# Batch normalization of a product on one core: the order of the scale and shift broadcasts, the place of the affine terms, and the statistics of the last tile

## The chip, the cores and the metric

The kernel runs on 1 core of one Trainium2 chip. The metric is the device time of one execution in microseconds (us). A profiled execution also has a span, from its first to its last instruction; all times inside the program below are counted from the start of that span.

## The reference

```
x: (16, 512, 1024) f32   weight: (1024, 768) f32   gamma, beta: (768) f32   eps = 1e-5
y      = matmul(x, weight)                      # 8192 rows, 768 columns
mean   = mean(y over all rows);  var = var(y over all rows)      # per column
out    = gamma * (y - mean) / sqrt(var + eps) + beta             # f32
```

Nothing of the output can be written before all 8192 rows of a column have been multiplied, since mean and variance are taken over them. Written as `out = y * scale + shift`, each column needs two numbers: `scale = gamma / sqrt(var + eps)` and `shift = beta - mean * scale`.

## The kernel before, in words

**Tiling.** The 768 columns are six tiles of 128, numbered 0 to 5 (`nt`). The 8192 rows are sixteen chunks of 512 (`c`). Tiles 0 to 2 (`GA = 3`) are done together, in two layouts. In twelve chunks the rows stand on the partitions (`mm_rows`: 128 rows by 384 columns), and in the chunks `COLS = (0, 5, 10, 15)` the columns stand on the partitions (`mm`: 128 columns by 512 rows). Tiles 3 to 5 have columns on the partitions in all chunks; their first five chunks (`EARLY`) are multiplied while x is still being loaded, the other eleven after it.

**Stages.** Until about 127 us x is loaded, turned and multiplied for tiles 0 to 2. Then `affine_rows` works out scale and shift of tiles 0 to 2 on VectorE. For chunks in the row layout scale and shift have to lie along the free dimension, the same on all partitions: VectorE writes diagonal matrices (`affine_rows` those of scale, `shift_diag` those of shift), and `spread_rows(i)` multiplies a matrix of ones with them on TensorE. The result for `i = 0` stays in PSUM, that for `i = 1` is copied by ScalarE to `sum1`. Each pair of row blocks is then multiplied by scale on VectorE (`norm_rows`), shifted on GpSimd (`shift_rows`, which reads `sum1`) and stored (`store_rows`). Chunks with columns on the partitions are normalized in place in bf16 (`norm`, on VectorE or ScalarE), turned back by transposes on TensorE (`turn_y`, into `o_ps`), copied out by ScalarE (`out_copy`, into `ring` or, for tile 5, `o_sb`) and stored.

**Tiles 3 to 5.** While this goes on, TensorE multiplies the remaining eleven chunks of tile 3, then of tile 4, then of tile 5, in half units of four matmuls. Each unit of 512 rows is read twice from PSUM: `bn` takes its statistics on VectorE, `keep` copies it to SBUF in bf16 on ScalarE. After the last chunk of a tile `finish` makes scale and shift of it, and its sixteen chunks are normalized, turned and stored (`outputs`, `last_outputs`). A waiting list, `turns`, holds transposes: each matmul of `mm` is followed by one of them, and `out_copy` issues those still missing of its block.

**The last chunk of the last tile.** It is multiplied in two halves of 256 rows (`mm_half`), each with a PSUM bank, statistics (`bn_half`) and copy (`keep_half`) of its own. `sum_up` aggregates chunks 0 to 13 beforehand into the small tile `fin`, to which chunk 14 and the two halves add their records, so that `finish(5)` aggregates 21 numbers per partition.

**Order.** Every step is put down by `at(t, ...)` with a planned time t in us. The steps are then sorted by t, and `seq` ties each engine's instructions together in that order. So t is no time at which something runs: it sets only the order within each engine and within the queue of SP, which issues all stores. An instruction that waits holds everything behind it on its engine. `S` is the planned end of the first stage, `tr` the planned time of the next row pair, and `tk` that of the next chunk's transposes. The row pieces and output copies take their space one after another from `ring`, which has room for eight of 768 words.

Of the kernel before, what the change touches and what calls it, by code (L numbers as in the profile page):

```python
# [10 lines left out]
def kernel(  # L11
# [23 lines left out]
    nc = tc.nc  # L35
    f32 = mybir.dt.float32
    bf16 = mybir.dt.bfloat16
    AF = mybir.ActivationFunctionType
    ALU = mybir.AluOpType
# [5 lines left out]
    P = 128  # L45
    NT = N // P
    KQ = K // 4
    CH = 512
    RT = CH // P
    C = M // CH  # L50
    QR = 256
    QPC = CH // QR
    JW = KQ // 64
# [12 lines left out]
    singles = ctx.enter_context(tc.tile_pool(name="singles", bufs=1))  # L66
# [3 lines left out]
    psum = ctx.enter_context(tc.tile_pool(name="psum", bufs=8, space=bass.MemoryType.PSUM))  # L70
# [3 lines left out]
    def seq(bi):  # L74

        ins = bi.ins
        prev = last.get(ins.engine)
        if prev is not None:
            tc.add_manual_dep(
                ins, prev,  # L80
                mybir.DependencyInfo(mybir.DependencyClass.NoSync, mybir.DependencyReason.DATA),
                reason="order",
            )
        last[ins.engine] = ins.name
        return bi
# [4 lines left out]
    gamma_sb = singles.tile([P, NT], f32)  # L90
    beta_sb = singles.tile([P, NT], f32)
    scale = singles.tile([P, NT], f32)
    shift = singles.tile([P, NT], f32)
    ident = singles.tile([P, P], bf16)
    ring = singles.tile([P, RING], f32)
    w_sb = singles.tile([P, JW, 2, N], bf16)
    eps_sb = singles.tile([P, 1], f32)
# [10 lines left out]
    for acc in (sum1, sum2, sum3):  # L108
        seq(nc.vector.memset(acc, 0.0))
    stats = singles.tile([P, NT, C, 6], f32)  # L110
    fin = singles.tile([P, 21], f32)
    msq = singles.tile([P, GA], f32)
    mv = singles.tile([P, NT, 2], f32)
    std = singles.tile([P, NT], f32)
    tmp = singles.tile([P, NT], f32)
    rstd = singles.tile([P, 1], f32)
# [5 lines left out]
    xs, xT, py, ygrp, yrow, ops, ost, aff = {}, {}, {}, {}, {}, {}, {}, {}  # L122
# [168 lines left out]
    def y(nt, c):  # L291
        key, i = ((nt, c // GY), c % GY) if nt >= GA else ((0, c), nt)
        if key not in ygrp:
            y_sb = ypool.tile([P, GY, CH], bf16, tag="y")
            ygrp[key] = y_sb
        return ygrp[key][:, i]

    def bn(nt, c):
        if (nt, c) == (NT - 1, C - 2):
            seq(nc.vector.bn_stats(fin[:, 3:9], py[nt, c]))  # L300
            return
        i = c if nt >= GA else COLS.index(c)
        seq(nc.vector.bn_stats(stats[:, nt, i, :], py[nt, c]))  # L303

    def sum_up():

        seq(nc.vector.memset(fin[:, 0:1], float((C - 2) * CH)))
        seq(nc.vector.bn_aggr(fin[:, 1:3], stats[:, NT - 1, 0:C - 2, :]))
        seq(nc.vector.tensor_scalar(
            fin[:, 2:3], fin[:, 2:3], float((C - 2) * CH), None, op0=ALU.mult))  # L310

    def mm_half(q):
        y_ps = psum.tile([P, CH], f32, tag="b")
        py["half", q] = y_ps[:, 0:QR]
        for jw in range(JW):
            for e in range(2):
                seq(nc.tensor.matmul(  # L317
                    y_ps[:, 0:QR], w_sb[:, jw, e, (NT - 1) * P:NT * P],
                    xT[C - 1][:, jw, q * QR:(q + 1) * QR, e],
                    start=(jw == 0 and e == 0), stop=(jw == JW - 1 and e == 1),  # L320
                ))

    def bn_half(q):
        seq(nc.vector.bn_stats(fin[:, 9 + 6 * q:15 + 6 * q], py["half", q]))

    def keep_half(q):
        seq(nc.scalar.copy(y(NT - 1, C - 1)[:, q * QR:(q + 1) * QR], py.pop(("half", q))))

    def keep(nt, c):
        seq(nc.scalar.copy(y(nt, c), py.pop((nt, c))))  # L330

    def finish(nt):
        one = slice(nt, nt + 1)
        src = stats[:, nt, :, :] if nt < NT - 1 else fin
        seq(nc.vector.bn_aggr(mv[:, nt, :], src))
        seq(nc.scalar.activation(std[:, one], mv[:, nt, 1:2], AF.Sqrt, bias=eps_sb, scale=1.0))
        seq(nc.vector.scalar_tensor_tensor(
            tmp[:, one], mv[:, nt, 0:1], -1.0, gamma_sb[:, one], op0=ALU.mult, op1=ALU.mult,
        ))
        seq(nc.vector.reciprocal(rstd, std[:, one]))  # L340
        seq(nc.vector.tensor_mul(scale[:, one], rstd, gamma_sb[:, one]))
        seq(nc.vector.scalar_tensor_tensor(
            shift[:, one], tmp[:, one], rstd, beta_sb[:, one], op0=ALU.mult, op1=ALU.add,
        ))
# [51 lines left out]
    def at(t, fn, *args):  # L396
        events.append((t, len(events), fn, args))
# [31 lines left out]
    pe = 0.0  # L429
# [12 lines left out]
    def unit(nt, c, span, jws=range(JW)):  # L442
        nonlocal pe
        pe = max(pe, arrive[c * RT + RT - 1])
        at(pe, mm, nt, c, jws)
        pe += span
        if jws[-1] == JW - 1:
            at(pe + 0.2, bn, nt, c)
            at(pe + 1.0, keep, nt, c)
# [13 lines left out]
    pe = max(pe, arrive["w", 2])  # L463
# [15 lines left out]
            at(pe + 2.0, merge_rows)  # L479

    S = pe
    at(S + 0.9, affine_rows)
    at(S + 4.4, spread_rows, 0)
    for nt in range(GA):
        at(S + 2.4, norm, nt, 0, "dve")
    at(S + 2.5, shift_diag)
    at(S + 5.2, spread_rows, 1)
    ga = tuple(range(GA))
    tr, tk = S + 5.3, S + 3.9
    for c in range(C):  # L490
        if c in COLS:
            for nt in range(GA):
                if c:
                    at(tk - 3.4 + 0.8 * nt, norm, nt, c, "act")
            for s in range(0, RT, 2):
                at(tk + 0.7 * s, turn_y, ga, c * CH + s * P, 2)
                at(tk + 0.7 * s + 1.9, out_copy, ga, c * CH + s * P, "act")
                at(tk + 0.7 * s + 2.7, store, ga, c * CH + s * P, 2)
            tk += 9.6 if c else 8.6
        else:  # L500
            for s in range(0, RT, 2):
                at(tr, norm_rows, c, s)
                at(tr + 1.1, shift_rows, c, s)
                at(tr + 3.0, store_rows, c, s)
                tr += 1.85

    def outputs(nt, t0, step):
        for b in range(C // 2):
            tb = t0 + step * b
            for i in range(2):  # L510
                at(tb - 2.2 + 0.5 * i, norm, nt, 2 * b + i, "act" if tb < tr + 2.0 and i == 0 else "dve")
            at(tb, turn_y, (nt,), 2 * b * CH, 2 * RT)
            at(tb + 2.2, out_copy, (nt,), 2 * b * CH, "act")
            at(tb + 2.3, store, (nt,), 2 * b * CH, 2 * RT)

    def last_outputs(nt, t0):

        for c in range(C):
            tb = t0 + 0.6 * c
            at(tb - 1.2, norm, nt, c, "dve")  # L520
            at(tb, turn_y, (nt,), c * CH, RT)
            at(tb + 0.5, out_copy, (nt,), c * CH, "act", True)
            at(tb + 0.6, store, (nt,), c * CH, RT)

    halves = [range(JW // 2), range(JW // 2, JW)]
    for nt in range(GA, NT):
        for c in range(EARLY, C):
            if (nt, c) == (NT - 1, C - 1):
                for q in range(QPC):
                    at(pe, mm_half, q)  # L530
                    pe += 0.9
                    at(pe + 0.2, bn_half, q)
                    at(pe + (0.4 if q == 0 else 1.0), keep_half, q)
                at(pe - 2.4, sum_up)
                continue
            for jws in halves:
                unit(nt, c, MM_US / 2 + (0.12 if nt == GA else 0.17), jws)
        at(pe + 0.55, finish, nt)
        if nt == GA:
            outputs(nt, S + 41.0, 2.0)  # L540
        elif nt < NT - 1:
            outputs(nt, pe + 4.6, 1.85)
        else:
            last_outputs(nt, pe + 3.0)
# [39 lines left out]
```

## Time and profile before

| what | value |
|---|---|
| time, median of 3 runs (lowest to highest) | 223.25 us (222.83 to 223.74) |
| the profiled execution: its own time, and its span | 223.25 us, 221.5 us |
| TensorE matmul busy | 199.8 us (90%) |
| VectorE busy | 156.3 us (71%) |
| GpSimd busy | 134.4 us (61%) |
| ScalarE busy | 119.9 us (54%) |
| HBM read and written | 36.71 MB and 25.17 MB |

The profile is read so. PE is TensorE, DVE VectorE, ACT ScalarE, POOL GpSimd, SP the engine whose queue issues the stores. A line of a timeline gives the start and the duration in us, the engine, the line of the kernel, the operation, the tile written and the tiles read, and the count if alike instructions are merged (then the duration goes from the first start to the last end). In brackets stands the idle time of the engine before it and what ended it. A table of slices cuts the span into 40 equal parts of 5.5 us; each digit is a busy share in tenths. The busy share of an engine is an average over stages with different limits, so the stages are looked at one by one.

### The profile page before, as it was taken

To read this page: it belongs to the slowest core of one execution; us is meant where nothing else is said; L and a number is where in the kernel's file an instruction comes from. 1 tells how busy PE (TensorE), PEld (TensorE's weight loads), DVE (VectorE), ACT (ScalarE), POOL (GpSimd) and SP (SyncE) were. 2 spreads that over 40 slices of the span, in tenths; PEclk is the share of its full clock that TensorE was granted. 3 is DMA by queue.
4 is the path that set the end of the run, shared out by engine and by line. 5 is a ranking of instruction groups with operands and counts; after the bars stand their busy time and mean duration, and the time that the engine had idled before them with its cause. 6 is when DMAs were issued, how large, how long until landed. Compare 5 with 4: busy or idle time off the path is not lost.

```text
span 221.5 us, 3438 instructions
## 1 busy us (share of the span) xinstructions
PE 199.8 (90%) x1162; PEld 105.0 (47%) x1178; DVE 156.3 (71%) x268; ACT 119.9 (54%) x221; POOL 134.4 (61%) x153
## 2 busy tenths in 40 slices
PE   7997999999999999999999979999999988996600
PEld 2452455554544566646665534444444545654400
DVE  3221978886988789998554287889989999738500
ACT  2000463544543476646766225685766978986920
POOL 8787686878674799935569003999899951000000
PEclk9999999999999999999999999999999999999965
DMA  5999999999999999991000001886769899999996
GB/s 60 168 184 179 183 196 196 197 197 196 196 190 197 195 196 196 198 194 16 0 4 0 0 0 37 322 331 240 285 240 361 305 363 323 323 347 319 280 287 202
DMA packets 70161, 43.75 MB, mean 198 GB/s; under 512 B 4096, under 2 KB 69632, under 8 KB 70144
## 3 DMA queue, kind: packets, MB, share of 16 engines
q0 software_dynamic: 34624, 18.36, 60.7%
q1 hardware_dynamic: 35520, 25.18, 35.4%
q8 instruction: 9, 0.15, 0.3%
q14 instruction: 8, 0.07, 0.1%
HBM read 36.71 MB, written 25.17 MB: 279 GB/s over the span
## 4 chain that ended last, share of the span: by engine, by line
PE 63%; DVE 10%; POOL 8%; DMA 6%; issue 4%; ACT 3%; ACTq 0%; DVEq 0%; POOLq 0%
PE y_ps L191 30%; PE y_ps L181 28%; POOL ring L281 6%; PE o_ps L369 3%; ACT o_sb L382 3%; DMA w_sb<-in_weight_dram 3%; DVE stats L303 2%; DMA ring<-in_x_dram 2%; DVE ring L275 2%; DVE y_sb L353 2%; POOL w_sb L144 2%; DMA out_dram<-ring 1%; POOL ring L157 1%; PE y_ps L317 1%; PE a_ps L267 1%
## 5 line engine op out<-in xcount | busy, mean ns | idle before, releaser
L191 PE MATMUL y_ps<-xT_sb,w_sb 128*128 128x512 bf16 (+1 forms) x469 | 115.8, 382 | 2.6 <-DMA w_sb<-in_weight_dram 1.6
L191 PEld LDWEIGHTS <-w_sb 128*128 128x128 bf16 x484 | 46.2, 96 | 59.4 <-issue 2.6
L330 ACT CAST y_sb<-y_ps 128x512 bf16<-128x512 f32 x59 | 34.8, 590 | 54.2 <-DVE stats L303 52.3
L181 PE MATMUL y_ps<-w_sb,xT_sb 128*128 128x384 bf16 x384 | 63.4, 326 | 0.0
L281 POOL TENSOR_TENSOR ring<-ring,sum 128x768 f32<-128x768 f32 x24 | 43.6, 1844 | 17.9 <-ACT sum L269 14.0
L303 DVE BATCH_NORM_STATS2 stats<-y_ps 128x6 f32<-128x512 f32 x58 | 39.2, 684 | 19.9 <-PE y_ps L191 19.7
L157 POOL DMA_DIRECT2D ring<-in_x_dram x72 | 45.3, 635 | 12.5 <-DVE xT_sb L169 6.6
L181 PEld LDWEIGHTS <-xT_sb 128*128 128x128 bf16 x384 | 37.5, 98 | 25.6
L207 POOL TENSOR_TENSOR sum<-sum,sq_sb 128x384 f32<-128x384 f32 x38 | 38.3, 1007 | 18.0 <-ACT sq_sb L203 16.8
L169 DVE STREAM_TRANSPOSE xT_sb<-ring 128x1024 f32<-128x1024 f32 (+1 forms) x34 | 39.5, 1168 | 13.6 <-DMA ring<-in_x_dram 13.5
L369 PE MATMUL o_ps<-ident,y_sb 128*128 128x128 bf16 x240 | 37.2, 219 | 4.8 <-DVE y_sb L353 4.6
L210 DVE TENSOR_TENSOR sum<-y_ps,sum 128x384 f32<-128x384 f32 x48 | 26.1, 544 | 14.2 <-ACT sq_sb L203 13.4
L203 ACT ACTIVATE sq_sb<-y_ps 128x384 f32<-128x384 f32 x48 | 23.4, 492 | 15.0 <-PE y_ps L181 11.8
L216 ACT CAST y_sb<-y_ps 128x384 bf16<-128x384 f32 x48 | 22.8, 476 | 7.8 <-DVE sum L210 7.4
L382 ACT CAST ring<-o_ps 128x1024 f32<-128x1024 bf16 (+1 forms) x24 | 22.4, 952 | 4.9 <-PE o_ps L369 3.2
L369 PEld LDWEIGHTS <-y_sb 128*128 128x128 bf16 x240 | 19.1, 97 | 9.7 <-DVE y_sb L353 6.5
L275 DVE TENSOR_TENSOR ring<-y_sb,a_ps 128x768 f32<-128x768 bf16 x24 | 22.4, 939 | 0.2 <-PE a_ps L267 0.2
L353 DVE TENSOR_SCALAR y_sb<-y_sb,scale,shift 128x512 bf16<-128x512 bf16 x43 | 17.3, 460 | 0.0
L348 ACT ACTIVATE y_sb<-y_sb,shift,scale 128x512 bf16<-128x512 bf16 x17 | 13.3, 813 | 0.1
L150 PE MATMUL idle_ps<-idle_sb 128*128 128x512 bf16 x37 | 11.2, 473 | 1.2 <-DVE idle_sb L100 1.2
L382 ACT CAST o_sb<-o_ps 128x512 f32<-128x512 bf16 x16 | 7.9, 673 | 1.2 <-PE o_ps L369 1.2
L150 PEld LDWEIGHTS <-idle_sb 128*128 128x128 bf16 x38 | 4.3, 117 | 7.5 <-issue 3.8
(54 smaller groups left out, 42.3 us busy)
## 6 DMA issues: line engine op xcount, KB each, us to landing
ring<-in_x_dram POOLq DMA_DIRECT2D x56, 256.0 KB, 8.6
out_dram<-ring SPq DMA_DIRECT2D x32, 384.0 KB, 2.9
out_dram<-ring SPq DMA_DIRECT2D x16, 512.0 KB, 5.9
out_dram<-o_sb SPq DMA_DIRECT2D x16, 256.0 KB, 3.6
ring<-in_x_dram POOLq DMA_DIRECT2D x16, 128.0 KB, 5.4
w_sb<-in_weight_dram POOLq DMA_DIRECT2D x8, 96.0 KB, 4.7
w_sb<-in_weight_dram POOLq DMA_DIRECT2D x4, 192.0 KB, 5.9
gamma_sb<-in_gamma_dram SPq DMA_DIRECT2D x6, 0.5 KB, 4.7
```

Source lines behind the costliest of these rows:

```text
L157: seq(nc.gpsimd.dma_start(x_bf[32 * i:32 * i + 32], src[:, :, KQ * i:KQ * (i + 1)]))
L169: seq(nc.vector.transpose(dst[:, half, :, jw0:jw1], src[:, :, jw0:jw1]))
L181: seq(nc.tensor.matmul(y_ps, xT[c][:, jw, s * P:(s + 1) * P, e], w_sb[:, jw, e, 0:NA], start=(jw == 0 and e == 0), stop=(jw == JW - 1 and ...
L191: seq(nc.tensor.matmul(y_ps, w_sb[:, jw, e, nt * P:(nt + 1) * P], xT[c][:, jw, q0 * QR:q1 * QR, e], start=(jw == 0 and e == 0 and q0 == 0) ...
L207: seq(eng.tensor_add(acc, acc, py.pop(("sq", c, s))))
L210: seq(nc.vector.tensor_add(sum1, py["row", c, s][:, 0:NA], sum1))
L275: seq(nc.vector.tensor_mul(o_sb, yrow[c][:, s:s + 2], aff[0][:, None, :].to_broadcast([P, 2, NA]),))
L281: seq(nc.gpsimd.tensor_add(o_sb, o_sb, sum1[:, None, :].to_broadcast([P, 2, NA])))
L303: seq(nc.vector.bn_stats(stats[:, nt, i, :], py[nt, c]))
L330: seq(nc.scalar.copy(y(nt, c), py.pop((nt, c))))
L369: seq(nc.tensor.transpose(dst, src, ident))
L382: seq(nc.scalar.copy(o_sb, src))
```

## The change

Three things are changed. First, around `S`: `shift_diag` comes before the normalization of chunk 0 in VectorE's order, the two broadcasts `spread_rows` have only one half unit of products between them, the transposes of chunk 0 come after both, row products and shifts are planned 0.6 us earlier, and the transposes of the other chunks in `COLS` 1.0 us later. Second, `finish` of tiles 3 and 4 (the fourth and fifth) is split: `finish_var` does the aggregate, the square root and the reciprocal, and `finish_affine` works out scale and shift in three operations on ScalarE, planned 1.05 us behind it. They use the negated gamma, made once beforehand by `negate_gamma`. Third, the last chunk of the last tile is multiplied, read and kept as one unit like the others, and `finish(5)` aggregates sixteen records; `fin`, `sum_up` and the three functions for halves are gone. One consequence is not seen in the diff: `outputs` gives a normalization to ScalarE only while its planned time is under `tr + 2.0`, and with the smaller `tr` chunk 2 of tile 4 goes to VectorE.

```diff
--- before.py
+++ after.py
@@ -108,7 +108,8 @@
     for acc in (sum1, sum2, sum3):
         seq(nc.vector.memset(acc, 0.0))
     stats = singles.tile([P, NT, C, 6], f32)
-    fin = singles.tile([P, 21], f32)
+    ngamma = singles.tile([P, NT], f32)
+    nscale = singles.tile([P, 1], f32)
     msq = singles.tile([P, GA], f32)
     mv = singles.tile([P, NT, 2], f32)
     std = singles.tile([P, NT], f32)
@@ -296,43 +297,31 @@
         return ygrp[key][:, i]
 
     def bn(nt, c):
-        if (nt, c) == (NT - 1, C - 2):
-            seq(nc.vector.bn_stats(fin[:, 3:9], py[nt, c]))
-            return
         i = c if nt >= GA else COLS.index(c)
         seq(nc.vector.bn_stats(stats[:, nt, i, :], py[nt, c]))
 
-    def sum_up():
-
-        seq(nc.vector.memset(fin[:, 0:1], float((C - 2) * CH)))
-        seq(nc.vector.bn_aggr(fin[:, 1:3], stats[:, NT - 1, 0:C - 2, :]))
-        seq(nc.vector.tensor_scalar(
-            fin[:, 2:3], fin[:, 2:3], float((C - 2) * CH), None, op0=ALU.mult))
-
-    def mm_half(q):
-        y_ps = psum.tile([P, CH], f32, tag="b")
-        py["half", q] = y_ps[:, 0:QR]
-        for jw in range(JW):
-            for e in range(2):
-                seq(nc.tensor.matmul(
-                    y_ps[:, 0:QR], w_sb[:, jw, e, (NT - 1) * P:NT * P],
-                    xT[C - 1][:, jw, q * QR:(q + 1) * QR, e],
-                    start=(jw == 0 and e == 0), stop=(jw == JW - 1 and e == 1),
-                ))
-
-    def bn_half(q):
-        seq(nc.vector.bn_stats(fin[:, 9 + 6 * q:15 + 6 * q], py["half", q]))
-
-    def keep_half(q):
-        seq(nc.scalar.copy(y(NT - 1, C - 1)[:, q * QR:(q + 1) * QR], py.pop(("half", q))))
-
     def keep(nt, c):
         seq(nc.scalar.copy(y(nt, c), py.pop((nt, c))))
 
+    def negate_gamma():
+        seq(nc.vector.tensor_scalar(ngamma, gamma_sb, -1.0, None, op0=ALU.mult))
+
+    def finish_var(nt):
+        one = slice(nt, nt + 1)
+        seq(nc.vector.bn_aggr(mv[:, nt, :], stats[:, nt, :, :]))
+        seq(nc.scalar.activation(std[:, one], mv[:, nt, 1:2], AF.Sqrt, bias=eps_sb, scale=1.0))
+        seq(nc.vector.reciprocal(rstd, std[:, one]))
+
+    def finish_affine(nt):
+        one = slice(nt, nt + 1)
+        seq(nc.scalar.activation(nscale, rstd, AF.Identity, scale=ngamma[:, one]))
+        seq(nc.scalar.activation(scale[:, one], rstd, AF.Identity, scale=gamma_sb[:, one]))
+        seq(nc.scalar.activation(
+            shift[:, one], mv[:, nt, 0:1], AF.Identity, bias=beta_sb[:, one], scale=nscale))
+
     def finish(nt):
         one = slice(nt, nt + 1)
-        src = stats[:, nt, :, :] if nt < NT - 1 else fin
-        seq(nc.vector.bn_aggr(mv[:, nt, :], src))
+        seq(nc.vector.bn_aggr(mv[:, nt, :], stats[:, nt, :, :]))
         seq(nc.scalar.activation(std[:, one], mv[:, nt, 1:2], AF.Sqrt, bias=eps_sb, scale=1.0))
         seq(nc.vector.scalar_tensor_tensor(
             tmp[:, one], mv[:, nt, 0:1], -1.0, gamma_sb[:, one], op0=ALU.mult, op1=ALU.mult,
@@ -479,14 +468,15 @@
             at(pe + 2.0, merge_rows)
 
     S = pe
+    at(S - 30.0, negate_gamma)
     at(S + 0.9, affine_rows)
+    at(S + 2.4, shift_diag)
     at(S + 4.4, spread_rows, 0)
+    at(S + 5.6, spread_rows, 1)
     for nt in range(GA):
-        at(S + 2.4, norm, nt, 0, "dve")
-    at(S + 2.5, shift_diag)
-    at(S + 5.2, spread_rows, 1)
+        at(S + 5.0, norm, nt, 0, "dve")
     ga = tuple(range(GA))
-    tr, tk = S + 5.3, S + 3.9
+    tr, tk = S + 4.7, S + 6.3
     for c in range(C):
         if c in COLS:
             for nt in range(GA):
@@ -496,7 +486,7 @@
                 at(tk + 0.7 * s, turn_y, ga, c * CH + s * P, 2)
                 at(tk + 0.7 * s + 1.9, out_copy, ga, c * CH + s * P, "act")
                 at(tk + 0.7 * s + 2.7, store, ga, c * CH + s * P, 2)
-            tk += 9.6 if c else 8.6
+            tk += 9.6 if c else 7.2
         else:
             for s in range(0, RT, 2):
                 at(tr, norm_rows, c, s)
@@ -525,17 +515,13 @@
     halves = [range(JW // 2), range(JW // 2, JW)]
     for nt in range(GA, NT):
         for c in range(EARLY, C):
-            if (nt, c) == (NT - 1, C - 1):
-                for q in range(QPC):
-                    at(pe, mm_half, q)
-                    pe += 0.9
-                    at(pe + 0.2, bn_half, q)
-                    at(pe + (0.4 if q == 0 else 1.0), keep_half, q)
-                at(pe - 2.4, sum_up)
-                continue
             for jws in halves:
                 unit(nt, c, MM_US / 2 + (0.12 if nt == GA else 0.17), jws)
-        at(pe + 0.55, finish, nt)
+        if nt < NT - 1:
+            at(pe + 0.55, finish_var, nt)
+            at(pe + 1.6, finish_affine, nt)
+        else:
+            at(pe + 0.55, finish, nt)
         if nt == GA:
             outputs(nt, S + 41.0, 2.0)
         elif nt < NT - 1:
```

## The prediction

> **What bounds the kernel now.** I read the page first, then the busy time by stage, the timelines of TensorE, VectorE, GpSimd and ScalarE from 125 us on, and the stores at the end. The page, rows of slices:
>
> ```profile
> PE   7997999999999999999999979999999988996600
> DVE  3221978886988789998554287889989999738500
> ACT  2000463544543476646766225685766978986920
> POOL 8787686878674799935569003999899951000000
> PEclk9999999999999999999999999999999999999965
> DMA  5999999999999999991000001886769899999996
> ```
>
> Each digit is 5.5 us. TensorE is full from slice 1 to slice 35 with dips, at a full clock, so until the last products (201.1 us) the kernel runs at TensorE's pace; after that only stores are left. The change touches nothing of weight before 127 us. So the question is where TensorE stands still after 127 us, and what follows its last product. TensorE's timeline (start, us, operation, in brackets the idle time before it and its releaser):
>
> ```profile
> 130.53 0.39 PE L191 MATMUL y_ps<-xT_sb,w_sb 128*128 128x512 bf16 x1
> 132.10 0.23 PE L369 MATMUL o_ps<-ident,y_sb 128*128 128x128 bf16 x1 [1.19 <-DVE y_sb L353]
> ...
> 180.78 0.23 PE L369 MATMUL o_ps<-ident,y_sb 128*128 128x128 bf16 x1 [0.68 <-DVE y_sb L353]
> ...
> 184.02 0.68 PE L369 MATMUL o_ps<-ident,y_sb 128*128 128x128 bf16 x5 [0.60 <-DVE y_sb L353]
> ```
>
> All three waits are a transpose standing in TensorE's order before VectorE has normalized its tile: 1.19 + 0.68 + 0.60 = 2.47 us. Matmul ends are modelled; by the pitch of matmuls (0.23 us from start to start) the losses are 1.34, 0.85 and 0.76, together 2.95. I take the recorded 2.47 and keep 2.95 as the other end. VectorE's timeline at the ends of tiles 3 and 4 shows why it is late at the second and third:
>
> ```profile
> 152.13 0.59 DVE L335 BATCH_NORM_AGGREGATE mv<-stats 128x2 f32<-128x96 f32 x1
> 152.76 0.16 DVE L337 SCALAR_TENSOR_TENSOR tmp<-mv,gamma_sb 128x1 f32<-128x1 f32 x1
> 153.08 0.16 DVE L340 RECIPROCAL rstd<-std 128x1 f32<-128x1 f32 x1 [0.17 <-ACT std L336]
> 153.28 1.42 DVE L341 TENSOR_TENSOR scale<-rstd,gamma_sb 128x1 f32<-128x1 f32 x1
> ...
> 174.64 1.18 DVE L337 SCALAR_TENSOR_TENSOR tmp<-mv,gamma_sb 128x1 f32<-128x1 f32 x1
> 175.75 0.15 DVE L340 RECIPROCAL rstd<-std 128x1 f32<-128x1 f32 x1
> 175.93 1.69 DVE L341 TENSOR_TENSOR scale<-rstd,gamma_sb 128x1 f32<-128x1 f32 x1
> 177.54 0.21 DVE L342 SCALAR_TENSOR_TENSOR shift<-tmp,rstd,beta_sb 128x1 f32<-128x1 f32 x1
> ...
> 179.15 1.90 DVE L353 TENSOR_SCALAR y_sb<-y_sb,scale,shift 128x512 bf16<-128x512 bf16 x2
> ```
>
> Operations on one element per partition take 0.16 us, or 1.2 to 1.7. GpSimd's own timeline:
>
> ```profile
> 155.78 21.83 POOL L281 TENSOR_TENSOR ring<-ring,sum 128x768 f32<-128x768 f32 x12 [1.09 <-DVE ring L275]
> 178.75 1.82 POOL L281 TENSOR_TENSOR ring<-ring,sum 128x768 f32<-128x768 f32 x1 [1.14 <-ACT y_sb L348]
> ```
>
> Its adds end every 1.82 us: 155.78 + 11 x 1.82 = 175.80, where the stalled `tmp` ends (175.82); 177.61, where the stalled `scale` ends (177.62). The two normalizations at 179.15 take 1.90 us for a usual 0.72, and finish just after the add that ends at 180.57. So some VectorE operations stand until GpSimd's add is through. The reciprocal does not: 0.16 us at 153.08, inside an add. From 166 to 190 us VectorE has no idle time, so these stalls reach the transposes.
>
> The end, in steps of 0.55 us from 200 us, and the first store of the last tile on SP's queue:
>
> ```profile
> GB/s 362 326 334 344 350 345 346 342 55 202 296 290 293 299 279 308 290 286 292 276 302 285 286 294 267 303 284 283 292 269 301 283 287 288 288 271 33 0 0 0
> ...
> 204.23 13.31 SPq L387 DMA_DIRECT2D out_dram<-o_sb  x16
> ```
>
> Tile 4's stores drain at 204.4; 0.6 us is nearly empty; then 16 stores run at some 288 GB/s to 219.8, and the span ends at 221.5. What sets the end is thus the first store of the last tile, as long as tile 4's drain stays ahead of it.
>
> **The change part by part.** The sum is made against the profiled execution: 223.25 us, span 221.5, 1.75 around it. It equals the median of the runs shown (223.25), so it needs no correction.
>
> *Head, 127 to 137 us.* Chunk 0's transposes go behind both broadcasts; TensorE instead does three more products of its half unit (to 131.44) and the first broadcast, whose diagonal is ready at 130.85. The 1.19 wait is gone if nothing else is late. VectorE, by present pitches: statistics to 131.65, shift diagonals (0.59) to 132.24, statistics (0.61) to 132.85, the first row product (0.86) to 133.71, three normalizations (0.32 each) starting at 133.71, 134.02 and 134.34. TensorE: broadcast 131.44 to 132.08 (0.64, as from 134.91 to 135.55), a half unit to 132.99, the second broadcast to 133.63, a half unit without transposes to 134.54; the first transpose is at 134.77, after its input (134.05). **Minus 1.19.**
>
> What is near: GpSimd's first add starts 1.40 us after the second broadcast now (134.91, 136.31), so at 134.39, against 134.34 for the third normalization. If the add comes first, that normalization waits. From the pair at 179.15 (the next instruction starts at 180.96, less 2 x 0.33 gives 180.30, 0.27 before the add's recorded end) it gets through at about 135.9 and ends at 136.2, with the third transpose due at 135.3: 0.9 us. I take 0, since VectorE is ahead by the rows, and keep 0.9.
> The Trainium skill, "SBUF — State Buffer", section "Who interferes with whom", says that a VectorE `tensor_scalar` in its two-port mode and a GpSimd instruction exclude each other, and that whoever issues first blocks the other for its whole instruction. The trace agrees on the block but shows it ending some 0.3 us before the recorded end. By the rule the wait would be to 136.2 and cost 1.2 instead of 0.9; this speaks against putting the normalizations next to the first add.
>
> *GpSimd.* Its first add moves from 136.31 to about 134.4, 1.9 us earlier. Its idle 1.09 at 155 us waits for a row product behind the stalled `scale`. With 24 adds at 1.82 from 134.4 it ends near 178.1 instead of 183.8, if rows come in time; the row stores follow. That frees DMA time before tile 4's stores.
>
> *Tiles 3 and 4.* On VectorE, aggregate to the next row product is now 152.13 to 154.76 = 2.63 us and 174.03 to 177.67 = 3.64. What remains is aggregate, the square root's wait and the reciprocal: 152.13 to 153.28 = 1.15 us each. It saves 1.48 and 2.49. VectorE also takes one normalization over from ScalarE (tile 4, chunk 2; it falls below the changed limit on `tr`): plus 0.33. Net 2.2 us at tile 4, and fewer stalls after GpSimd's earlier end. TensorE's 0.68 and 0.60 are both smaller than that. **Minus 1.28**; bounds 0 and minus 1.61 by pitch. ScalarE takes three one-element operations per tile: the square root (0.30, next start after 0.19) is the nearest row, so 0.6 to 0.9 per tile. At tile 4 the normalization given away (0.81) pays for it; at tile 3 ScalarE idled 1.50 before the square root. Nothing. If that cover is gone, 0.9 falls on the output copies.
> Behind the square root on ScalarE are a copy to SBUF, the affine terms, a normalization and an output copy; behind the reciprocal on VectorE the next row product.
>
> *Last tile.* TensorE's time for the last unit does not change (eight of 0.23 against sixteen of 0.11). Statistics of 512 columns are 0.69 instead of 0.43, the aggregate of 16 records 0.58 instead of 0.25. Both lie on the path to the first store. **Plus 0.59.** `sum_up` was hidden: nothing. Transposes, copies and stores are as before.
>
> *Small edits.* `negate_gamma` (0.15) at about 97 us lies in a stage that TensorE sets: nothing, at most 0.15. Chunks 5, 10 and 15 are turned one half unit later in the order, which TensorE's earlier arrival offsets; SP's queue then sees row stores earlier relative to theirs. DMA is at 53% to 87% in most slices there, so nothing, bounds minus 0.3 and plus 0.3.
>
> *Drain.* The first late store moves 1.88 earlier, data from 205.0 to 203.1. Tile 4's drain, 204.4, must come 1.3 earlier. The head alone moves everything by 1.19, and 3 to 4 row stores of 384 KB (about 1.1 us each at 345 GB/s) leave the time after 177 us. I take it as met.
>
> Sum: -1.19 - 1.28 + 0.59 = **-1.88**, 223.25 to **221.4 us**. By pitch -1.34 - 1.61 + 0.59 = -2.36, 220.9.
>
> **The rivals.** *Race at the head lost:* the add takes the port first, 0.9 of the gain goes: -1.0, 222.3. For it: 0.05 us of lead. Against: both sides share most of their history.
> *Second half does not pay:* TensorE meets the waits again, or the drain stays at 204.4 (then only the empty 0.6 is won): -1.19 + 0.59 = -0.60, or -0.6: 222.65. For it: ScalarE and DMA are both full from 186 to 196 us. Against: ScalarE's idle 0.66, 0.39 and 0.93 between 179 and 186 wait for VectorE's statistics and go with it.
> *Slower: the square root holds ScalarE's queue at tile 4.* Ahead of the aggregate VectorE now has a normalization, which an add can hold by 1.5, and a row product (0.86, formerly behind). Then the aggregate ends near 175.8 and ScalarE, ready at 174.0, stands 1.8 us; after square root, reciprocal, copy, affine terms, normalization and output copy, tile 4's first normalization ends at 179.7 instead of 178.6. TensorE then is 1.1 later than before, plus 0.59: +1.7, 224.9. It decides once that normalization ends later than 178.6. Against: the present stalls of the normalizations from 168 to 174 are under 0.1.
>
> **How the numbers follow.** A measurement here can tell about 0.5% (1.1 us) from no change. Forecast 0.58, with its own range 220.8 to 222.2; race lost 0.16; second half 0.13; slower 0.13. Faster takes nearly all of the forecast and the better end of the first rival: 0.62. Same: 0.25. Slower: 0.13. The range 220.7 to 223.3 takes in the forecast and the two middle rivals.
>
> **What would show it.** Right: no idle over 0.3 us before L369 near 132 to 136 and 178 to 184; GpSimd's first add near 134.4 and its last ending before 180; reciprocal at tile 4 within 1.3 us of the aggregate's start; last product near 198.6; 2.2 us from there to the first normalization (1.6 now). Wrong: a normalization of 1.5 us near 134; idle before the square root with output copies behind it; a drain that ends after 203.2.

## The result, and the profile after

The changed kernel takes 225.91 us (median of 6 runs, 225.01 to 226.85) against 223.15 us before: a ratio of 1.012, 95% interval 1.0091 to 1.0149. It is slower, by more than the 0.5% that can be told from no change. The profiled execution took 225.01 us with a span of 223.2 us, the lowest of the six; it is compared with the profiled 221.5 us of before, so it explains 1.7 us of the 2.8.

TensorE's timeline of after, only the instructions that waited:

```profile
175.04 0.23 PE L358 MATMUL o_ps<-ident,y_sb 128*128 128x128 bf16 x1 [0.50 <-DVE y_sb L342]
...
177.96 0.23 PE L358 MATMUL o_ps<-ident,y_sb 128*128 128x128 bf16 x1 [0.50 <-DVE y_sb L342]
...
181.48 0.23 PE L358 MATMUL o_ps<-ident,y_sb 128*128 128x128 bf16 x1 [2.23 <-ACT y_sb L337]
```

The wait of 1.19 us at the head is gone, as forecast. The two waits at tile 4 (0.68 and 0.60) have become three, of 0.50, 0.50 and 2.23. VectorE's timeline of after shows where they come from:

```profile
166.31 2.83 DVE L342 TENSOR_SCALAR y_sb<-y_sb,scale,shift 128x512 bf16<-128x512 bf16 x1
169.07 0.94 DVE L276 TENSOR_TENSOR ring<-y_sb,a_ps 128x768 f32<-128x768 bf16 x1
169.93 0.68 DVE L301 BATCH_NORM_STATS2 stats<-y_ps 128x6 f32<-128x512 f32 x1
170.54 1.53 DVE L342 TENSOR_SCALAR y_sb<-y_sb,scale,shift 128x512 bf16<-128x512 bf16 x1
171.99 0.94 DVE L276 TENSOR_TENSOR ring<-y_sb,a_ps 128x768 f32<-128x768 bf16 x1
...
173.46 1.52 DVE L342 TENSOR_SCALAR y_sb<-y_sb,scale,shift 128x512 bf16<-128x512 bf16 x1
...
176.38 1.53 DVE L342 TENSOR_SCALAR y_sb<-y_sb,scale,shift 128x512 bf16<-128x512 bf16 x1
...
178.69 0.58 DVE L311 BATCH_NORM_AGGREGATE mv<-stats 128x2 f32<-128x96 f32 x1
```

Before, these four normalizations of tile 3 took 0.40, 0.45, 0.45 and 0.40 us. The first two of them in VectorE's timeline of before:

```profile
168.18 0.40 DVE L353 TENSOR_SCALAR y_sb<-y_sb,scale,shift 128x512 bf16<-128x512 bf16 x1
...
169.97 0.45 DVE L353 TENSOR_SCALAR y_sb<-y_sb,scale,shift 128x512 bf16<-128x512 bf16 x1
```

GpSimd's timeline of after, beside VectorE's:

```profile
134.65 34.34 POOL L282 TENSOR_TENSOR ring<-ring,sum 128x768 f32<-128x768 f32 x19 [12.06 <-ACT sum L270]
170.09 1.83 POOL L282 TENSOR_TENSOR ring<-ring,sum 128x768 f32<-128x768 f32 x1 [1.09 <-DVE ring L276]
173.01 1.83 POOL L282 TENSOR_TENSOR ring<-ring,sum 128x768 f32<-128x768 f32 x1 [1.09 <-DVE ring L276]
```

Nineteen adds run without a pause. The normalization issued at 166.31 waits for the running one and lets one more pass. It ends at 169.14, when GpSimd has nothing left. From then on the engines take turns: row product (0.86), add, and a normalization that stands until the add is nearly through. A round takes 2.92 us (from 170.09 to 173.01) where TensorE needs 2.25. The aggregate of tile 4 comes at 178.69, formerly at 174.03, and on ScalarE:

```profile
179.30 0.29 ACT L312 ACTIVATE std<-mv,eps_sb 128x1 f32<-128x1 f32 x1 [3.53 <-DVE mv L311]
...
180.62 0.80 ACT L337 ACTIVATE y_sb<-y_sb,shift,scale 128x512 bf16<-128x512 bf16 x1
```

ScalarE stands 3.53 us before the square root; behind it in ScalarE's order is the normalization of 180.62, for which TensorE waits 2.23 us. By the planned times that is chunk 8 of tile 3: it needs nothing of tile 4, and stands behind the square root only by the order.

The sum of the profiled executions: the stage begins 0.27 later (the last statistics of the load stage start at 127.37, formerly 127.10), head -1.19, tile 4 +3.23 - 1.28 = +1.95, together +1.03; the last product ends 1.14 later (202.21 and 201.07). From there to the first normalization it is 2.24 instead of 1.64: +0.60. That makes 1.74, against 1.7 of span.

### The profile page after: what moved, and what is told of

Its sections match the earlier page's. It is cut to its first block, busy times and chain, and to the rows that moved or that the text cites. A ratio compares the mean times of both kernels' runs of the same rounds, so it can differ in the third digit from the quotient of the medians.

```text
span 223.2 us, 3421 instructions
## 1 busy us (share of the span) xinstructions
PE 199.1 (89%) x1154; PEld 103.9 (47%) x1170; DVE 156.2 (70%) x260; ACT 119.0 (53%) x225; POOL 134.2 (60%) x153
## 4 chain that ended last, share of the span: by engine, by line
PE 73%; DVE 8%; DMA 5%; ACT 4%; issue 3%; POOL 3%; DVEq 0%; ACTq 0%; POOLq 0%
PE y_ps L192 40%; PE y_ps L182 28%; DVE y_sb L342 3%; PE o_ps L358 3%; ACT o_sb L371 3%; DMA w_sb<-in_weight_dram 3%; DMA ring<-in_x_dram 2%; DVE ring L276 2%; DVE stats L301 2%; POOL w_sb L145 2%; POOL ring L158 1%; PE a_ps L268 1%; PE tot_ps L228 1%; ACT y_sb L337 0%; ACT y_sb L304 0%
## 5 line engine op out<-in xcount | busy, mean ns | idle before, releaser
L192 PE MATMUL y_ps<-xT_sb,w_sb 128*128 128x512 bf16 (+1 forms) x477 | 117.8, 382 | 3.5 <-DMA w_sb<-in_weight_dram 2.4
L192 PEld LDWEIGHTS <-w_sb 128*128 128x128 bf16 x492 | 46.9, 96 | 61.6 <-issue 4.3
L304 ACT CAST y_sb<-y_ps 128x512 bf16<-128x512 f32 x60 | 35.3, 588 | 54.0 <-DVE stats L301 52.1
L301 DVE BATCH_NORM_STATS2 stats<-y_ps 128x6 f32<-128x512 f32 x60 | 40.5, 685 | 21.3 <-PE y_ps L192 20.7
L358 PE MATMUL o_ps<-ident,y_sb 128*128 128x128 bf16 x240 | 36.7, 219 | 6.3 <-DVE y_sb L342 3.7
L342 DVE TENSOR_SCALAR y_sb<-y_sb,scale,shift 128x512 bf16<-128x512 bf16 x44 | 22.5, 569 | 0.0
L337 ACT ACTIVATE y_sb<-y_sb,shift,scale 128x512 bf16<-128x512 bf16 x16 | 12.6, 813 | 0.0
L151 PE MATMUL idle_ps<-idle_sb 128*128 128x512 bf16 x37 | 10.4, 445 | 1.2 <-DVE idle_sb L100 1.2
```

The costliest lines, as they stand in the source:

```text
L192: seq(nc.tensor.matmul(y_ps, w_sb[:, jw, e, nt * P:(nt + 1) * P], xT[c][:, jw, q0 * QR:q1 * QR, e], start=(jw == 0 and e == 0 and q0 == 0) ...
L342: seq((nc.vector if eng == "dve" else nc.gpsimd).tensor_scalar(y(nt, c), y(nt, c), scale[:, nt:nt + 1], shift[:, nt:nt + 1], op0=ALU.mult, ...
L358: seq(nc.tensor.transpose(dst, src, ident))
```

## The experiments

**Parts alone.** First theory (A): the normalizations of tile 3 stand behind the adds because GpSimd, started earlier, has used up its stock of row products. Rival (B): the operations added to ScalarE hold its queue.

*e1, the last chunk as one unit alone* (the diff's lines on `fin`, `sum_up` and the halves, nothing else).

> The kernel before, with only the last tile's last chunk done as one unit. All theories: statistics of 512 columns and an aggregate of 16 records lie between the last product and the first normalization, 2.2 us instead of 1.6 between them, so plus 0.6 us: about 223.8. If tile 4's drain sets the start of the last stores, nothing: 223.2.

Measured: 221.26 us, ratio 0.9905 (0.9871 to 0.9939). Neither expected time was right. The first normalization of the last tile is 0.6 us later from the last product, as expected; but the last sixteen stores take 10.58 us on SP's queue instead of 13.31. That has nothing to do with the statistics; it is settled below (e6 to e8).

*e2, the head alone* (the lines around `S`, `tr` and `tk`).

> The kernel before, with only the head changed (shift diagonals and both broadcasts ahead of chunk 0's normalizations and transposes). Theory A (VectorE's normalizations of tile 3 stand behind GpSimd's adds once GpSimd has used up its stock of row products; the head starts GpSimd 1.7 us earlier and so empties the stock): normalizations of 1.4 us or more at 165 to 178 us, idle of GpSimd of about 1.1 us before several late adds, time 223 to 225. Rival B (the affine terms on ScalarE cause it, the head is a gain): minus 1.2 us, about 222.0, and no idle of TensorE over 0.7 us at 174 to 184.

Measured: 222.06 us, 0.9948 (0.9922 to 0.9974). Rival B's number, though TensorE stood 1.00 us at 179.39, more than B's 0.7. Three of the four normalizations took 0.63, 0.45 and 0.45; the fourth 1.91.

*e3, the affine terms on ScalarE alone* (`negate_gamma`, `finish_var`, `finish_affine`).

> The kernel before, with only the affine terms of tiles 3 and 4 on ScalarE. Theory A with the head as trigger: tile 3's normalizations stay at 0.4 us, TensorE's idle of 0.68 and 0.60 shrinks, 222 to 223. Rival B (the square root and three more operations in ScalarE's order hold its output copies at tile 4): ScalarE idle over 2 us before the square root at tile 4, TensorE idle over 2 us behind it, 224.5 to 225.5.

Measured: 222.50 us, 0.9941 (0.9903 to 0.998), but from 220.80 to 225.51 in ten runs. In the profiled one (220.80) the normalizations took 0.98, 0.46, 0.45 and 0.45. By the medians neither part causes the loss alone; head and affine terms together do. Only the fastest of the ten runs of e3 was profiled, so whether normalizations were held in its runs of 224.29 and 225.51 is not shown.

*e4, the changed kernel with those normalizations on ScalarE.*

```diff
-  "act" if tb < tr + 2.0 and i == 0 else "dve"
+  "act" if tb < tr + 2.0 else "dve"
```

> The changed kernel, with those normalizations of tiles 3 and 4 that are planned while rows are still under way given to ScalarE alone instead of in turn to ScalarE and VectorE. Theory A: no two-port operation of VectorE stands beside an add any more; GpSimd's adds run on at 1.82 us, aggregate of tile 4 near 174.5 instead of 178.7, TensorE's idle 0.5, 0.5 and 2.2 goes except for under 0.5: 222 to 223, that is 3 us less than the changed kernel. Rival B (ScalarE's queue is the limit at tile 4): four more operations of 0.8 us there make it worse, 226 or more.

Measured: 222.75 us, 0.9984 (0.996 to 1.0009), 3.2 us less than the changed kernel. In the profiled execution (224.56, the slowest of ten) GpSimd ran 23 adds in 41.54 us without a pause, the aggregate came at 174.75, and TensorE waited 0.90 and 0.54 for ScalarE. ScalarE took more work and the kernel became faster, so B falls: the loss is in VectorE's normalizations beside the adds.

**What lets a normalization in.** *e5, more work for GpSimd.*

```diff
+    for i in range(4):
+        at(S + 20.0 + 2.0 * i, ballast)      # gpsimd.tensor_add(sum3, sum3, sum2)
```

> The changed kernel with four extra adds of 128x384 (1.0 us each) on GpSimd between the row adds from about 147 to 155 us; they change only a sum that is no longer read. Theory A (the stall needs an empty stock of row products: with two in stock each normalization of tile 3 finds the gap between two adds, with none it waits for a whole add and the next add waits for it): more work makes it faster. Normalizations of tile 3 at 0.5 us or less, aggregate of tile 4 near 175 instead of 178.7, TensorE's waits at 174 to 182 under 1.5 us together instead of 3.2, 223.0 to 224.5. Rival C (GpSimd is simply the slower engine, and all that delays it delays the stores): 4 us more on GpSimd, 226.5 to 230.

Measured: 227.92 us, 1.0203 (1.0156 to 1.025). VectorE's and GpSimd's timelines of e5:

```profile
165.21 6.20 DVE L345 TENSOR_SCALAR y_sb<-y_sb,scale,shift 128x512 bf16<-128x512 bf16 x1
```

```profile
156.90 14.35 POOL L285 TENSOR_TENSOR ring<-ring,sum 128x768 f32<-128x768 f32 x8
```

Three products were in stock when the normalization was issued, and it waited for the running add and all three: 6.20 us, to 171.41, just past the run's end at 171.25. Theory A falls: a stock makes the wait longer. The time lies in rival C's range, but C's reason, GpSimd's longer work by itself, is not what TensorE's timeline shows: TensorE stood 3.28 us for this normalization, and 2.22 us for one on ScalarE later.

*e9 and e10, the phase (how much of the running add is left when the normalization is issued).* One or two aggregates (0.58 us each) on VectorE right before the first normalization.

```diff
+    for _ in range(1):                       # e10: range(2)
+        at(S + 39.28, delay)                 # vector.bn_aggr(spare, stats[:, GA, :, :])
```

> The changed kernel with one aggregate of 0.58 us more on VectorE (into a spare tile) right before tile 3's first normalization there. In the changed kernel that normalization starts 0.89 us before the end of an add and waits until GpSimd has no row product left; in the kernel before it starts 0.19 us before an end and takes 0.40. Theory F (the phase decides: a normalization that comes in the last half microsecond of an add gets in between two adds, and the next ones keep that phase; one that comes earlier waits out the stock): with the added 0.58 it starts about 0.3 us before the end and all four take 0.5 us or less, aggregate of tile 4 near 175.5, TensorE's waits at 174 to 182 down from 3.2 to under 1.5, 223.0 to 224.5 us. Rival G (GpSimd's empty stock makes the two engines alternate whatever the phase): first normalization 2 us or more, the others 1.5, 225.9 to 226.5.

> The same with two such aggregates, 1.16 us: the normalization then starts 0.27 us inside the next add, the last one in stock. Theory F: it waits for this add's end (1.3 to 1.6 us) with no stock left, the two engines alternate as in the changed kernel: 225.5 to 226.8. If more delay alone helps (VectorE later, more products waiting): below 224.5.

Measured: e9 226.02 us, 1.0105 (1.0047 to 1.0163); e10 225.73 us, 1.0108 (1.0062 to 1.0154). In e9 the normalization started 0.38 us before an add's end (167.01, 167.39), nearer than the 0.48 of e2, and still let the next add pass (2.33 us, then 1.53 each). Theory F falls too; e10 went as it said, but tells nothing without e9. Rival G had the numbers of e9 right; but an empty stock is not the reason, since e3 had one product in stock as well and its normalization got in.

What remained in the profiles is how long GpSimd had been running without a pause. Read off the traces: the add that runs when the first normalization of tile 3 on VectorE is issued, counted from GpSimd's last idle time; the time left of this add; the row products in stock; and what the normalization took (0.40 with no add beside it). One later normalization, e2's fourth, is added.

| kernel | add since idle | left, us | stock | took, us |
|---|---|---|---|---|
| before | 7th | 0.19 | 2 | 0.40 |
| e2 | 7th | 0.48 | 2 | 0.63 |
| e2, its fourth | 11th | 1.76 | 1 | 1.91 |
| e3 | 12th | 0.83 | 1 | 0.98 |
| after | 18th | 0.89 | 1 | 2.83 |
| e9 | 18th | 0.38 | 1 | 2.33 |
| e5 | 20th (with the four small adds) | 0.73 | 3 | 6.20 |

The phase matters in one way. A normalization that came with 0.31 us or less left of an add hardly waited, however long GpSimd had run: all four of before (0.19 to 0.30 left, 0.40 to 0.45 us), and e3's second to fourth, in the 13th to 15th add (0.30 to 0.31 left, 0.45 to 0.46 us). One that came earlier had to wait, and there the length of the run parts the rows.

*i11, i16 and in_none, an idle time put in (theory H: after a long run of adds a normalization no longer gets in; an idle time renews that).* Small aggregates on VectorE that delay a row product of the changed kernel.

```diff
+    for _ in range(8):                       # i16: range(15), 32.40; in_none: range(6), 12.05
+        at(S + 23.15, delay)                 # vector.bn_aggr(spare, stats[:, 0, 0:4, :])
```

> The changed kernel with eight small aggregates (about 1.2 us together, into a spare tile) on VectorE ahead of row product 11, at about 152 us, where GpSimd has 0.2 us in hand: GpSimd stands idle for about 1 us there, as it does in the kernel before. Theory H (after a long run of adds without idle time a normalization no longer gets in between two of them; an idle time renews that): tile 3's normalizations of 1 us or less for the first and 0.5 for the others, TensorE's waits at 174 to 182 under 1.5 us together, 222.8 to 224.2. Rival (the head and the affine terms together do it in another way): as the changed kernel, 225.5 to 226.5.

> The same with fifteen aggregates (about 2.3 us) ahead of row product 16, at about 159 us, where 1.5 us are in hand: an idle time of about 0.7 us two adds before the first normalization. Theory H: it gets in, 222.8 to 224.5. Rival: 225.5 to 227.

> The same with six aggregates (about 0.9 us) ahead of row product 5, at about 140 us, where 1.3 us are in hand: a delay of VectorE without idle time of GpSimd. Theory H: as the changed kernel, normalizations of 1.5 us and more, 225.3 to 226.5. If a delay on VectorE by itself is what helps: under 224.5.

Measured: i11 220.78 us, 0.9908 (0.9876 to 0.9941); i16 222.06 us, 0.9974 (0.9943 to 1.0005); in_none 225.96, 226.58, 226.80 and one run of 220.73, for which no ratio is given. GpSimd's and VectorE's timelines of i11:

```profile
132.99 18.19 POOL L286 TENSOR_TENSOR ring<-ring,sum 128x768 f32<-128x768 f32 x10 [12.06 <-ACT sum L274]
153.23 25.42 POOL L286 TENSOR_TENSOR ring<-ring,sum 128x768 f32<-128x768 f32 x14 [2.05 <-DVE ring L280]
```

```profile
164.77 1.23 DVE L346 TENSOR_SCALAR y_sb<-y_sb,scale,shift 128x512 bf16<-128x512 bf16 x1
...
167.39 0.45 DVE L346 TENSOR_SCALAR y_sb<-y_sb,scale,shift 128x512 bf16<-128x512 bf16 x1
...
172.33 0.58 DVE L315 BATCH_NORM_AGGREGATE mv<-stats 128x2 f32<-128x96 f32 x1
```

A delay on VectorE that makes GpSimd idle for 2.05 us at its eleventh add takes 5.1 us off the changed kernel. The delays were twice what had been reckoned (2.33 us in i11, 4.43 in i16), and the times of both kernels lie below theory H's ranges. i11 is the changed kernel with eight small operations more, and by its ratio it takes 2.1 us less than before, where the prediction's sum was 1.88 less: once the normalizations get in, the rest of that sum holds. The first normalization came with 1.08 us of the 7th add left, more than any first one that had got in so far, and got in at that add's end. In i16 it came in the 3rd add, with 0.57 left, and took 0.72; the stock was one product, as in e9, where less was left (0.38) and the next add passed. In the profiled in_none (226.58) the delay happened to make a short idle time after all, 0.39 us before the fifth add, so that the normalization came in the 14th: it took 3.24, and the others 1.54. In these profiles, then, a normalization of tile 3 that has to wait gets in at the next end up to the 12th add (and, in i11, a later one in the 13th), and not from the 14th on as long as a product is in stock. The 14th is seen in in_none alone; without it the bound lies between the 13th and the 18th. e3, at the 12th, is also the kernel whose runs spread by 4.7 us. That the idle time makes the difference is shown by i11 and i16; what in GpSimd changes over a run of adds is not, and stays open. So does the single run of 220.73, which was not profiled; in_none, meant as a delay without an idle time, had a short one, so such a delay was not tested by itself.

**The stores.** The address of `o_sb` follows from the sizes of the small tiles ahead of it in SBUF: 62048 bytes into the partition before, 62016 in the changed kernel, 61952 in e1 (reckoned from the tiles; the profile shows no addresses). Only the last is a multiple of 256. Theory D was put to three kernels with an unused tile of the right size behind the small ones:

```diff
+    pad = singles.tile([P, 48], f32)         # e6: 192 bytes; e7: 160; e8: 96
```

> The changed kernel with 192 bytes per partition of unused tile behind the small tiles, so that the output tiles of the last tile start at a multiple of 256 bytes in SBUF (62208 instead of 62016). Theory D (the last stores run at 345 instead of 288 GB/s when their 512-byte rows start on such a multiple, as they happened to do in the kernel with the last chunk as one unit alone): stores of 10.6 us on SP's queue instead of 13.3, minus 2.0 to 2.3 us, 223.6 to 223.9. Rival E (the faster stores came from the last chunk's being one unit): no change, 225.9.

> The kernel before with 160 bytes of unused tile, output tiles of the last tile at 62208 instead of 62048. Theory D: minus 2.0 to 2.3 us, 221.0. Rival E: no change, 223.2.

> The kernel with only the last chunk as one unit and 96 bytes of unused tile in the place of the removed ones: output tiles at 62048 again. Theory D: the stores fall back to 288 GB/s and the plus 0.6 us of the longer statistics shows, 223.7 to 223.9. Rival E: 221.3 as without the unused tile.

Measured: e6 223.53 us, 1.0 (0.9972 to 1.0027), 2.4 less than the changed kernel; e7 221.56 us, 0.9893 (0.9832 to 0.9954); e8 223.73 us, 1.0029 (1.0005 to 1.0054). All three lie nearer to theory D's times (e6 223.6 to 223.9, e7 221.0, e8 223.7 to 223.9) than to rival E's, and so do the stores. The last stores on SP's queue, first of e7 and then of e8:

```profile
203.61 10.97 SPq L389 DMA_DIRECT2D out_dram<-o_sb  x16
```

```profile
204.17 13.45 SPq L360 DMA_DIRECT2D out_dram<-o_sb  x16
```

e8 also shows the last chunk's own price: +0.3% where +0.6 us had been expected (+0.27%).

**Better versions.** *e11: the head of the change and 160 bytes of padding.*

> The kernel before with the head of the change, and the output tiles of the last tile at 62208 by 160 bytes of unused tile; no affine terms on ScalarE, the last chunk in halves. All gains found so far without the loss: 222.1 of the head alone less 2.0 to 2.3 of the faster stores: 219.7 to 220.2, if the first normalization of tile 3 keeps its phase.

Measured: 219.34 us, 0.9815 (0.979 to 0.9839), the lowest median here and 0.4 us under what was expected. GpSimd's idle time of 1.36 us before its eleventh add is still there, left by a stalled `tmp` of tile 3, and the first normalization takes 0.66.

*e12: head, affine terms, halves, padding, and the normalizations on ScalarE.*

> Head and affine terms of the change, the last chunk in halves, output tiles at 62208, and all normalizations of tiles 3 and 4 that are planned while rows are under way on ScalarE, so that no two-port operation of VectorE stands beside an add until GpSimd is through. From 222.75 of the changed kernel with these normalizations on ScalarE: less 0.6 for the halves and 2.0 to 2.3 for the stores, 219.8 to 220.2. If ScalarE is the limit at 176 to 182 us it stays above 221.

Measured: 220.53 us, 0.9866 (0.9838 to 0.9894). No normalization of VectorE waits before GpSimd's last add. TensorE waits 0.89 and 0.54 for those on ScalarE; but e4, from which the estimate was made, had the same two waits (0.90 and 0.54), so they do not explain the 0.3 to 0.7 us over the estimate. What does is not shown.

## Why the prediction was wrong, step by step

**Head: right.** The 1.19 us went. GpSimd's first add came at 134.65, which is 134.38 with the stage's later begin taken off (134.39 forecast). The close race was won: the three normalizations took 1.06 us together. e2 alone measured -1.1 us.

**Affine terms, VectorE's side: right in itself.** Aggregate to next row product at tile 3 was 150.63 to 151.66, 1.03 us (1.15 forecast, 2.63 before). The three operations on ScalarE started 0.19 us apart and took 0.29, 0.28 and 0.38.

**Last tile: right.** +0.60 in the profile (+0.59 forecast), and e8.

**GpSimd and tile 4: wrong, and this is the step that failed.** The prediction reckoned that GpSimd, earlier and without its idle 1.09 at 155 us, would end near 178.1 and leave VectorE "fewer stalls". Its last add ended at 183.26, four normalizations of VectorE took 7.41 us where they had taken 1.70, and the term of -1.28 came out as +1.95. That idle time, made by a `scale` that stood behind an add, was what let the later normalizations in: put back in another place (i11, i16) it lets them in again. The head alone keeps one (1.36 us, before the eleventh add), the affine terms alone keep one (0.25, before the seventh); both together leave none between the first add and the nineteenth.

**The third rival was the right mechanism.** It had a normalization held by an add, a late aggregate and ScalarE standing before the square root: 224.9 us forecast, 225.01 in the profiled execution (225.91 in the median). It was given 0.13, because the stalls from 168 to 174 us were under 0.1. That reading was the mistake: 0.40 and 0.45 us beside adds that ran on were taken to mean that no add blocks these operations, while the pair at 179.15 in the same profile showed one that did. They were short because each was issued in the last 0.30 us of an add. That the rival's time comes so near is partly luck, for its own sizes were short: it let one normalization be held by 1.5 us, where four took 5.7 longer than before (7.41 - 1.70), so that ScalarE idled 3.53 instead of 1.8 and tile 4's first normalization ended at 183.04 instead of 179.7.

**The rule weighed against the change.** The Trainium skill, "SBUF — State Buffer", section "Who interferes with whom", has the blocked instruction wait for the whole of the other. The traces agree that a normalization is blocked, and differ in the amount: in e5 it waited through the running add and three more that had not begun when it was issued. The prediction applied the rule at the head and not at tile 3, where it mattered.

## What to carry to other kernels

Where two engines exclude each other, a short stall beside a busy neighbour is no proof of safety: look for the instance that waited long, and ask what the neighbour's schedule must look like for the short ones. Taking idle time out of an engine that is not the bottleneck can cost more than it saves; removing two stalls that are each a gain can be a loss. And compare the rate of the last stores after any edit that adds or removes a small tile: what lies behind it in SBUF moves.

## What the runs showed of the hardware

- An operation of VectorE that waits for GpSimd's adds can be passed over by adds that follow without a pause: 2.83 us with one in stock (after), 6.20 us with three (e5). With an idle time of GpSimd few adds back, it got in at the next end (i11: 1.23 us, in the 7th add).
- The block ends before the add's recorded end: a normalization issued 0.30 us before that end took 0.45 us, one issued 0.25 us before it 0.40 us, which is what it takes with no add beside it.
- VectorE's reciprocal of one element per partition is not held by an add: 0.15 to 0.17 us within one in the profiles here that have one there, where a `scale` beside it took 1.42.
- Stores of 512-byte rows ran at about 288 GB/s from SBUF addresses 96 or 64 bytes off a multiple of 256, and at about 345 GB/s from a multiple: 13.3 to 13.5 and 10.0 to 11.1 us for the sixteen issues. The Trainium skill, "DMA: Bandwidth & Descriptors", section "How a descriptor splits into AXI transactions", fits: worked out by its rule, a piece of 512 bytes that starts on a multiple of 256 makes two transactions, and any other takes a third. It gives no rate for it; the runs do, and show no transactions.
